# Batch normalisation, streamed: loads freed of their wait on VectorE while each store stays held for its predecessor's landing, VectorE's two instructions fused, ScalarE's share cut from 2048 to 1408 columns

One core of a Trainium2 chip. The metric is the device time of one execution in microseconds (us); lower is better.

## The reference

```python
# x: (32, 256, 128, 128) float32; gamma, beta, running_mean, running_var: (256,)
return gamma * (x - mean) / np.sqrt(var + eps) + beta      # per channel
```

Each element is read, scaled and shifted by two numbers of its channel, and written. 537 MB go in and 537 MB come out.

## The kernel before

x is cut into 64 tiles of 128 channels x 16384 columns (8 MB; 64 KB in each of 128 partitions). There are three buffers of a tile each (192 KB per partition together). SyncEngine issues the loads, ScalarE the stores, so they are on two DMA queues; VectorE scales columns 0 to 14335 in place, in two instructions, and ScalarE the last 2048. The parts that matter (`...` marks cuts):

```python
NBUF = 3
STEP, VCOLS, VLAST = 2560, 14336, 9216
...
for i in range(1, NT):                       # SyncEngine: loads
    s, turn = i % NBUF, i // NBUF
    if turn:
        nc.sync.wait_ge(stored[s], 16 * turn)            # store i-3 has left the buffer
    inst = nc.sync.dma_start(out=bufs[s][:], in_=xr[i]).then_inc(loaded[s], 16)
    if turn:
        inst._wait_ge(vdone, 2 * (i - 1) + 1)            # tile i-1 landed, its first 2560 columns done
...
for i in range(1, NT):                       # VectorE
    vector_part(i, 0, STEP)._wait_ge(*landed(i))
    vector_part(i, STEP, VLAST if i == last else VCOLS)
for i in range(last):                        # ScalarE: its columns, then the store
    nc.scalar.wait_ge(vdone, 2 * (i + 1))
    inst = scalar_part(i, VCOLS)
    if i:                                                # store i-1 has landed
        inst._wait_ge(stored[(i - 1) % NBUF], 16 * ((i - 1) // NBUF + 1))
    store(i)                                             # waits for scalar_part(i)
```

So there are two **holds**: a load is held for a piece of VectorE work on the tile loaded before it, a store for the landing of the store before it.

## Time and profile before

| | before |
|---|---|
| time, median of 3 runs | 2484.97 us |
| span of the profiled run | 2483.3 us |
| one tile (one load and one store), steady state | 38.68 us |
| moved | 1073.85 MB, 432 GB/s |

The prediction below shows the lines that carry the argument. Two more are needed for comparison, the DMA issues of the page (size, count, median us from issue to landing):

```profile
out_dram<-t ACTq DMA_DIRECT2D x64, 36.5
t<-in_x_dram SPq DMA_DIRECT2D x63, 37.0
```

Both are shorter than a tile's 38.68 us, so each queue is empty for a moment in every tile.

### The profile page before, as it was taken

The numbers are of one execution on the slowest core, as the hardware profiler recorded it, in microseconds if no ns is written. First come the engines' busy times: TensorE is split into PE (matmuls) and PEld (weight loads), VectorE is DVE, ScalarE is ACT, GpSimd is POOL, SyncE is SP. The second block draws the span as 40 slices with busy tenths as digits, with TensorE's granted clock in tenths as the row PEclk, the third lists the DMA queues.
The fourth block names the chain that finished last, engine by engine and source line by source line (L and its number), as shares of the span: only waits on it lengthen the run. The fifth ranks groups of instructions, "written<-read, shape, count | busy, mean of one in ns | idle before, by whom it ended". The sixth has DMA issues, their size and how long they took to land.

```text
span 2483.3 us, 516 instructions
## 1 busy us (share of the span) xinstructions
DVE 508.8 (20%) x139; ACT 139.8 (6%) x66; POOL 0.2 (0%) x4
## 2 busy tenths in 40 slices
DVE  3122121221212212122121221212212122121220
ACT  0000000000000000000000000000000000000001
POOL 0000000000000000000000000000000000000000
DMA  9999999999999999999999999999999999999999
GB/s 415 430 439 434 428 436 436 435 433 430 432 433 438 430 432 433 435 424 437 437 428 436 438 436 429 437 435 430 436 437 436 430 437 435 429 437 435 433 433 408
DMA packets 18708, 1073.85 MB, mean 432 GB/s; under 512 B 2128, under 2 KB 2192, under 8 KB 2192
## 3 DMA queue, kind: packets, MB, share of 16 engines
q1 hardware_dynamic: 9488, 536.94, 50.1%
q10 hardware_dynamic: 9216, 536.88, 49.9%
q14 instruction: 4, 0.03, 0.0%
HBM read 536.94 MB, written 536.87 MB: 432 GB/s over the span
## 4 chain that ended last, share of the span: by engine, by line
DMA 93%; DVE 4%; another core or an unknown queue 1%; ACT 0%; issue 0%; SPq 0%; DVEq 0%
DMA t<-in_x_dram 93%; DVE t L130 4%; ACT t L141 0%; SPq L91 0%; DVE rows L89 0%; SPq L95 0%; DVE eps_t L107 0%; DVEq L198 0%; SPq L70 0%
## 5 line engine op out<-in xcount | busy, mean ns | idle before, releaser
L130 DVE TENSOR_SCALAR t<-t,scale_t,shift_t 128x11776 f32<-128x11776 f32 (+2 forms) x128 | 505.3, 3989 | 1930.4 <-DMA t<-in_x_dram 1930.2
L141 ACT ACTIVATE t<-t,shift_t,scale_t 128x2048 f32<-128x2048 f32 x64 | 138.2, 2159 | 2299.3 <-DMA out_dram<-t 2276.6
L108 DVE STREAM_TRANSPOSE turned<-rows 32x1024 f32<-32x1024 f32 x1 | 1.2, 1233 | 12.5 <-DMA rows<-in_running_mean_dram 12.5
L115 ACT ACT_TABLE_LOAD x1 | 1.3, 1283 | 0.9 <-SPq L70 0.9
L89 DVE MEMSET rows<- 32x1024 f32 x1 | 0.9, 912 | 1.2 <-SPq L70 1.2
L115 ACT ACTIVATE std_t<-par,eps_t 128x2 f32<-128x2 f32 x1 | 0.3, 296 | 14.7 <-DVE par L113 14.7
L113 DVE COPY par<-turned 32x8 f32<-32x8 f32 x4 | 0.6, 161 | 0.1
L122 DVE RECIPROCAL rstd_t<-std_t 128x2 f32<-128x2 f32 x1 | 0.2, 166 | 0.4 <-ACT std_t L115 0.4
L125 DVE TENSOR_TENSOR shift_t<-par,ms_t 128x2 f32<-128x2 f32 x1 | 0.2, 161 | 0.0
L124 DVE TENSOR_TENSOR ms_t<-par,scale_t 128x2 f32<-128x2 f32 x1 | 0.2, 161 | 0.0
L123 DVE TENSOR_TENSOR scale_t<-par,rstd_t 128x2 f32<-128x2 f32 x1 | 0.2, 160 | 0.0
L187 POOL MEMSET const-bfloat16-1.0<- 128x1 bf16 x1 | 0.1, 101 | 0.0
L187 POOL MEMSET const-uint8-127<- 128x1 uint8 x1 | 0.1, 101 | 0.0
L187 POOL MEMSET const-float32-0.0<- 128x1 f32 x1 | 0.1, 98 | 0.2 <-issue 0.2
L187 POOL MEMSET const-float32-1.0<- 128x1 f32 x1 | 0.1, 98 | 0.0
L107 DVE MEMSET eps_t<- 128x1 f32 x1 | 0.1, 59 | 0.1
## 6 DMA issues: line engine op xcount, KB each, us to landing
t<-in_x_dram SPq DMA_DIRECT2D x2, 4096.0 KB, 16.5
out_dram<-t ACTq DMA_DIRECT2D x64, 36.5
t<-in_x_dram SPq DMA_DIRECT2D x63, 37.0
rows<-in_running_var_dram SPq DMA_DIRECT2D x1, 16.0 KB, 11.3
rows<-in_gamma_dram SPq DMA_DIRECT2D x1, 16.0 KB, 11.1
rows<-in_beta_dram SPq DMA_DIRECT2D x1, 16.0 KB, 10.9
rows<-in_running_mean_dram SPq DMA_DIRECT2D x1, 16.0 KB, 11.3
```

The costliest lines, as they stand in the source:

```text
L89: zeroed = step(nc.vector.memset(rows[:], 0.0))
L107: step(nc.vector.memset(eps_t[:], eps))
L108: step(nc.vector.transpose(out=turned[:], in_=rows[:]), fetched, 16 * NPAR)
L113: placed = step(nc.vector.tensor_copy(out=flat[q * B : (q + 1) * B], in_=blocks[:, :, q, 0]))
L115: nc.scalar.activation(out=std_t[:], in_=var_t, func=mybir.ActivationFunctionType.Sqrt, bias=eps_t[:], scale=1.0,)._wait_ge(vec, placed).t ...
L122: step(nc.vector.reciprocal(out=rstd_t[:], in_=std_t[:]), act, 1)
L123: step(nc.vector.tensor_mul(out=scale_t[:], in0=gamma_t, in1=rstd_t[:]))
L124: step(nc.vector.tensor_mul(out=ms_t[:], in0=mean_t, in1=scale_t[:]))
L125: ready = step(nc.vector.tensor_sub(out=shift_t[:], in0=beta_t, in1=ms_t[:]))
L130: return nc.vector.tensor_scalar(out=t[:, first:end], in0=t[:, first:end], scalar1=scale_t[:, cb : cb + 1], scalar2=shift_t[:, cb : cb + 1 ...
L141: return nc.scalar.activation(out=t[:, first:], in_=t[:, first:], func=mybir.ActivationFunctionType.Identity, bias=shift_t[:, cb : cb + 1] ...
L187: nc = _bacc.Bacc("TRN2", target_bir_lowering=False, num_devices=1)
```

## The change

It frees the loads of the wait on VectorE (985 us of SyncEngine's waiting), shortens the ScalarE pass that lies between two stores, and fuses VectorE's two instructions into one.

```diff
-STEP = 2560
-VCOLS = 14336
+VCOLS = 14976
...
-            if turn:
-                nc.sync.wait_ge(stored[s], 16 * turn)
             inst = nc.sync.dma_start(out=bufs[s][:], in_=xr[i]).then_inc(loaded[s], 16)
             if turn:
-                inst._wait_ge(vdone, 2 * (i - 1) + 1)
+                inst._wait_ge(stored[s], 16 * turn)
...
-            vector_part(i, 0, STEP)._wait_ge(*landed(i))
-            vector_part(i, STEP, VLAST if i == last else VCOLS)
+            vector_part(i, 0, VLAST if i == last else VCOLS)._wait_ge(*landed(i))
         for i in range(last):
-            nc.scalar.wait_ge(vdone, 2 * (i + 1))
+            nc.scalar.wait_ge(vdone, i + 2)
```

More of the change, by code (lines that the diff above doesn't have):

```diff
@@ L167 @@
         scalar_part(last, VLAST)._wait_ge(*landed(last))
-        nc.scalar.wait_ge(vdone, 2 * NT)
+        nc.scalar.wait_ge(vdone, NT + 1)
         store(last)
```

## The prediction

> **What bounds the kernel now.** I read the page first: what the engines and the DMA engines are busy with.
>
> ```profile
> DVE 508.8 (20%) x139; ACT 139.8 (6%) x66; POOL 0.2 (0%) x4
> ...
> DMA  9999999999999999999999999999999999999999
> ...
> HBM read 536.94 MB, written 536.87 MB: 432 GB/s over the span
> ...
> DMA t<-in_x_dram 93%; DVE t L130 4%; ACT t L141 0%; SPq L91 0%; DVE rows L89 0%; SPq L95 0%; DVE eps_t L107 0%; DVEq L198 0%; SPq L70 0%
> ```
>
> VectorE and ScalarE are mostly idle, and no slice of the DMA row falls below nine tenths. The chain that ended last names loads (93%) and the short VectorE piece between two loads (4%). That 4% looks like a loss to be won back. Whether it is one, the timeline of a steady stretch and the table of stretches tell:
>
> ```profile
> 1197.34 2.09 ACT L141 ACTIVATE t<-t,shift_t,scale_t 128x2048 f32<-128x2048 f32 x1 [36.50 <-DMA out_dram<-t]
> 1199.47 0.34 ACTq L154 DMA_DIRECT2D out_dram<-t  x1
> 1211.90 7.93 DVE L130 TENSOR_SCALAR t<-t,scale_t,shift_t 128x2560 f32<-128x2560 f32 x2 [30.69 <-DMA t<-in_x_dram]
> 1213.55 77.61 SPq L102 DMA_DIRECT2D t<-in_x_dram  x3
> 1236.02 2.09 ACT L141 ACTIVATE t<-t,shift_t,scale_t 128x2048 f32<-128x2048 f32 x1 [36.58 <-DMA out_dram<-t]
> ```
> ```profile
> 158.30:2399.00 2240.70, 460.26 (x116) 121.37 (x58) 0.00 (x0) 1.00 1.00 434
> ```
>
> From one ScalarE pass to the next is 1236.02 - 1197.34 = 38.68 us (38.64 averaged over the neighbours): one tile loaded and one stored. Both queues have a pause per tile: the store is released at 1199.47, the next load at 1213.55, 14 us apart, so one queue runs alone in the other's pause. In the records of single packets a tile is 8 packets of 64 KB per DMA engine and direction; a packet takes an engine 2.414 us from start to start, whether loads, stores or both are queued, and the next starts when it ends. 16 x 2.414 = 38.63 us, the whole period. So the DMA engines have no idle time at all in the steady state (the table's DMA share over 2240 us is 1.00, at 434 GB/s); the 4% of VectorE in the chain is hidden. 64 x 38.63 = 2472 us of the 2483 us span; the rest is start and end. **There is nothing above about 0.5% to win, whatever the waits are; a new idle moment of the DMA engines is a loss in full.**
>
> **What the Trainium skill says.** (1) "DMA: Bandwidth & Descriptors", section "Queues, rings and completion order": each DMA engine takes turns between queues, packet by packet. The packet records agree: where both have work, each engine alternates one load and one store packet. (2) The same page, "Why a DMA increments its semaphore by 16 and not by 1": the 16 engines finish independently and only the full count means that all has landed. Here one store's 16 completion marks lay from 1192.5 to 1197.0 us, 4.5 us apart, and ScalarE began 0.33 us after the last. (3) The same page, "Where 436 GB/s comes from", gives 435.2 GB/s as the ceiling; the 434 here agrees. (4) The same page, "Anatomy of one DMA", puts about 2 us of fixed cost on a DMA and says that any wait is done by the issuing sequencer, before dispatch. The trace shows the parts of it that matter here, which I use instead.
>
> **The change part by part.**
>
> *VectorE and ScalarE work.* Two VectorE instructions per tile become one of 14976 columns. From the groups by shape, 2560 columns take 1.613 us and 11776 take 6.408 us, so 0.520 ns per column and about 8.07 us for 14976, against 8.02 us now. ScalarE's 2048 columns take 2.093 us and the single 7168 take 6.360 us, so 0.833 ns per column: 1408 columns take 1.56 us, 0.53 us less. Neither engine bounds anything, and a tile will have been scaled about a period before its store. Worth nothing while the DMA engines are full.
>
> *The loads' pause goes.* A load now waits only for the store that empties its buffer (load i for store i-3), no longer for 2560 columns of the tile before it. That wait costs 985 us in total on SyncEngine (61 times 16.15 us), but it is not a loss: it is what puts loads half a turn away from stores.
>
> ```profile
> SPq L101 <- DMA out_dram<-t: 1398.1, 61, 68.8
> SPq L102 <- DVE t L130: 985.0, 61, 16.2
> ```
>
> *What this makes of the order.* Load i+3 and store i+1 are now released by the same event, the last landing of store i; the load at once, the store 1.56 us of ScalarE later. So loads get a lead in every turn, of ScalarE's time plus the store's start-up: in the trace the first store packet moves 3.6 us or more after its issue when loads are queued. That is about 1.6 + 3.6 = 5 us or two packets, in which loads run alone; then the queues alternate; the loads, 8 packets like the stores, run out first; the last two or so store packets go alone. When the slowest engine ends the store, nothing is queued anywhere: three buffers, of which one is just stored and two are loaded. **Both queues are empty until the landing has been seen and a new load has started.** A lead of a few loads at the start does not save it: load 2 has about 2 to 3 packets left per engine when store 0 ends (store 0's first packets move at 35 us, when 5 to 6 of load 1's 8 have gone; the remaining 10 to 11 against store 0's 8), and each pause of the stores consumes 2 to 3. It is gone by the end of store 1 or 2.
>
> *The size of the idle moment.* Last completion mark to seen: 0.33 us in the steady state, 0.36 us at the end of the kernel. Issue to moving bytes in an idle machine: only the first load shows it. Issued at 0.95 us, its first packet starts at 1.95 us, the slowest engine's at 2.56 us, and the first packets take 1.6 to 2.4 us where later ones of their size (32 KB) take 1.21 us. The slowest two engines end their first packet at 4.20 and 4.52 us, that is 2.04 and 2.36 us later than a packet's time after the issue. The table of stretches shows the silence:
>
> ```profile
> 0.95:1.90 0.95, 0.69 (x1) 0.95 (x1) 0.00 (x0) 1.00 0.00 0
> 1.90:2.90 1.00, 0.28 (x2) 0.28 (x1) 0.00 (x0) 1.00 1.86 524
> ```
>
> The slowest engine sets each turn. So 0.36 + 0.02 + (2.04 to 2.36) = 2.4 to 2.7 us; I take 2.45, as a first issue is probably slower than a later one. New period: 38.63 + 2.45 = 41.1 us.
>
> *Number and sum.* Stores 1 or 2 to 60 each release a load that way: 59 times 2.45 = 145 us. After store 61 no load is left, and store 62 comes after ScalarE as well: 0.36 + 1.56 + 2.1 = 4 us. The end (store 63 queued behind store 62) and the start (1408 instead of 2048 columns, -0.2 us) stay. 2485 + 145 + 4 = 2634 us; rounded 2632.
>
> **The rivals.**
>
> *The queues stay full.* If the loads kept a backlog over the end of each store, the idle moment would be covered and the time would stay at 2480 to 2490 us. For it: at the start there is a backlog, and the engines are up to 4.5 us out of step, so some have work when others are done. Against it: the alternation is one to one, the backlog can only shrink while stores alone pause, and a load can't be issued before a store frees its buffer. A strong preference of the DMA engines for stores would be needed; the packet records show none. I give it 7%.
>
> *The idle moment is longer.* The engines' being out of step could be paid too: if, in a turn, one engine is a whole packet (2.4 us) later than the others, everything waits for it, and the period would be 38.63 + 4.9 = 43.5 us, 2484 + 60 x 4.9 = 2780 us. For it: 4.5 us between first and last completion mark now. Against it: that spread is of whole packets by order of turns, and in the new order every engine has the same 16 packets between two common starts, with only the start's 0.6 us between engines. 7%.
>
> *The idle moment is shorter.* If a warm issue moves bytes in 1 us and the first packet costs no more than later ones, 0.36 + 1.0 + 0.1 = 1.5 us: 59 x 1.5 + 3 = 91 us, 2576 us. Quite possible; it sets my lower end.
>
> *A gain.* Two waits fewer in the chain might seem to give back 4%, 2390 us. That needs 452 GB/s over the whole span; no packet in the trace goes faster than 2.414 us. 1%.
>
> **Range and chances.** The shorter idle moment gives 2576 and a longer one of 3.4 us (start-up as measured plus another microsecond of packet fill) gives 2690. Range 2572 to 2690. Faster 1%, within 2% (up to 2535 us) 8%, slower 91%.
>
> **What the changed profile would show.** Right: the DMA share of a steady stretch near 0.94 and about 408 GB/s instead of 434; ScalarE passes about 41.1 us apart; each load issued within 0.1 us of the ScalarE pass beginning, both right after a store's landing; loads landing some packets before the store of the same turn, and then about 2.4 us in which no packet starts; SyncEngine waiting for stores alone. Wrong: passes 38.6 us apart with the share at 1.00 (first rival: loads still under way when a store ends), or 43 us apart (second rival: completion marks of a store still 4 us apart). The whole argument fails if store packets get more than every second turn while loads are queued, or if loads end after the stores.

## The result

The changed kernel takes **2710.69 us** (median of 4 runs, 2709.51 to 2713.30) against 2484.26 us: ratio 1.0916, 95% interval 1.0900 to 1.0932. (Ratios here are the mean time of one kernel's fast runs over that of the other's in the same rounds, so not quite the ratio of the medians.) The prediction had the direction and the mechanism, but 2632 us, with 2690 at the upper end.

The timeline of a steady stretch of the changed kernel (columns: start, duration, engine, line, operation; in brackets the idle time before it and what ended that):

```profile
1225.13 8.08 DVE L125 TENSOR_SCALAR t<-t,scale_t,shift_t 128x14976 f32<-128x14976 f32 x1 [34.95 <-DMA t<-in_x_dram]
1227.53 85.42 SPq L97 DMA_DIRECT2D t<-in_x_dram  x3
1227.54 1.56 ACT L136 ACTIVATE t<-t,shift_t,scale_t 128x1408 f32<-128x1408 f32 x1 [41.44 <-DMA out_dram<-t]
1229.13 0.34 ACTq L149 DMA_DIRECT2D out_dram<-t  x1
1268.01 8.08 DVE L125 TENSOR_SCALAR t<-t,scale_t,shift_t 128x14976 f32<-128x14976 f32 x1 [34.80 <-DMA t<-in_x_dram]
1270.42 1.56 ACT L136 ACTIVATE t<-t,shift_t,scale_t 128x1408 f32<-128x1408 f32 x1 [41.32 <-DMA out_dram<-t]
```

The load at 1227.53 and ScalarE's pass at 1227.54 are released by one landing. Before, they were 14 to 16 us apart. The load of the same turn had landed at 1225.13, when VectorE begins: 2.4 us before that store. At 1225.13 each DMA engine was at its last store packet; in the packet records the last of these ended at 1227.16, and no packet of the next tile started before 1228.48.

SyncEngine's waits (us in total, times, longest), the table of stretches (its last three columns are TensorE clock, DMA share, GB/s) and the page's DMA issues agree:

```profile
SPq L97 <- DMA out_dram<-t: 2596.7, 61, 66.9
```
```profile
158.30:2399.00 2240.70, 428.20 (x53) 82.74 (x53) 0.00 (x0) 1.00 0.95 396
```
```profile
out_dram<-t ACTq DMA_DIRECT2D x64, 40.6
t<-in_x_dram SPq DMA_DIRECT2D x63, 39.8
```

Note that the share fell by 5% and the rate by 9% (434 to 396 GB/s). **A busy share does not show that packets take longer**, and longer packets are the part of the loss that the prediction missed. The trace's records of single packets split a tile's time, for each DMA engine, into packets at the steady 2.414 us, what load packets took beyond 2.418 us (store packets took none), and time in which the engine had none (means over tiles 2 to 59, us):

| kernel | one tile | 16 packets x 2.414 | slow load packets | idle |
|---|---|---|---|---|
| before | 38.68 | 38.63 | 0.05 | 0.0 |
| changed | 42.31 | 38.63 | 1.66 | 2.0 |

The last completion mark of a store (each DMA engine writes one, a record of 4 bytes, when its share is done) is followed 1.33 us later by the first load packet on the first engine. The first load packet of a tile takes 3.08 us in the mean, the second 3.40, the other six 2.42.

The books close. Up to the landing of store 61 the changed kernel lost 231.7 us: 59 tiles by 3.63 = 214 us; 4.8 and 14.6 us more than a tile before in the first two periods, when the order collapses; -1.9 us at the first store. From there to the end it takes 43.5 us against 49.6, as its last load has long landed. 231.7 - 6.1 = 225.6 us, the difference of the spans.

### The profile page after: what moved, and what is told of

Same layout as the page of the kernel before. It is cut to its first block, busy times and chain, and to the rows that moved or that the text cites. A ratio compares the mean times of both kernels' runs of the same rounds, so it can differ in the third digit from the quotient of the medians.

```text
span 2708.9 us, 392 instructions
## 1 busy us (share of the span) xinstructions
DVE 517.9 (19%) x76; ACT 106.3 (4%) x66; POOL 0.2 (0%) x4
## 2 busy tenths in 40 slices
DMA packets 18708, 1073.85 MB, mean 396 GB/s; under 512 B 2128, under 2 KB 2192, under 8 KB 2192
## 3 DMA queue, kind: packets, MB, share of 16 engines
q1 hardware_dynamic: 9488, 536.94, 49.6%
## 4 chain that ended last, share of the span: by engine, by line
DMA 93%; ACT 4%; another core or an unknown queue 1%; DVE 0%; issue 0%; SPq 0%; ACTq 0%; DVEq 0%
DMA out_dram<-t 90%; ACT t L136 4%; DMA t<-in_x_dram 3%; DVE t L125 0%; SPq L90 0%; DVE rows L88 0%; ACTq L149 0%; DVE eps_t L102 0%; DVEq L192 0%; ACTq L156 0%; SPq L69 0%
## 5 line engine op out<-in xcount | busy, mean ns | idle before, releaser
L125 DVE TENSOR_SCALAR t<-t,scale_t,shift_t 128x14976 f32<-128x14976 f32 (+2 forms) x65 | 514.4, 7913 | 2136.4 <-DMA t<-in_x_dram 2136.3
L136 ACT ACTIVATE t<-t,shift_t,scale_t 128x1408 f32<-128x1408 f32 x64 | 104.7, 1636 | 2552.5 <-DMA out_dram<-t 2541.3
```

The lines of the kernel that those rows point to most:

```text
L125: return nc.vector.tensor_scalar(out=t[:, first:end], in0=t[:, first:end], scalar1=scale_t[:, cb : cb + 1], scalar2=shift_t[:, cb : cb + 1 ...
L136: return nc.scalar.activation(out=t[:, first:], in_=t[:, first:], func=mybir.ActivationFunctionType.Identity, bias=shift_t[:, cb : cb + 1] ...
```

## The experiments

**Theory (coinciding releases):** one event, the landing of a store, now releases both the next load and, after ScalarE, the next store; both queues run empty together once per tile, and the DMA engines, which are the bound, stand still. **Rivals:** the new split of work, or the fused VectorE instruction, costs; ScalarE's pass is on the path, as the chain of the changed kernel has 4% of it; three buffers are too few. Every timed run below is against the kernel before of its own rounds.

### 1. cols_only: the split of columns alone

```diff
 # kernel before
-VCOLS = 14336
+VCOLS = 14976
```

> The kernel before with only the column split of the change (VectorE ends at column 14976, ScalarE takes 1408); both waits stay. Theory of empty queues (the period grew because loads and stores are now released by one event, so that both queues run empty once per tile): within 0.5% of the kernel before, 2475 to 2495 us, period 38.6 us. Rival, that the new split of the work costs or gains time by itself: more than 1% off, towards 2710 us if it is the whole cause.

2487.46 us, ratio 1.0009 (0.9994 to 1.0024). The split is nothing.

### 2. load_wait_only: the load's wait alone

```diff
 # kernel before
-            if turn:
-                nc.sync.wait_ge(stored[s], 16 * turn)
...
-                inst._wait_ge(vdone, 2 * (i - 1) + 1)
+                inst._wait_ge(stored[s], 16 * turn)
```

> The kernel before with only the load's wait changed: no wait for 2560 columns of the preceding tile, the landing of the store of three tiles earlier alone; two VectorE instructions and 2048 ScalarE columns stay. Theory of empty queues: the whole loss is here, 2690 to 2730 us, period about 42.3 us. Rival, that the fused VectorE instruction or the new split carries a part: clearly less than 2690 us.

2716.51 us, ratio 1.0936 (1.0920 to 1.0953); 42.39 us per tile, of which 1.64 us slow load packets and 2.05 us idle. The whole loss is in this one wait, with VectorE's two instructions and ScalarE's 2048 columns still there.

### 3. store_late: ScalarE's pass 5.2 us longer

```diff
 # changed kernel
-VCOLS = 14976
+VCOLS = 8704
```

> The changed kernel with 7680 instead of 1408 ScalarE columns per tile, so about 6.8 instead of 1.56 us between the landing of a store and the issue of the next one; VectorE's pass shrinks to about 4.8 us. Theory of empty queues: the store's pause is covered by the load that starts at once, so the period stays at 42.3 us (2690 to 2730 us) if the slow first two load packets (3.08 and 3.40 us instead of 2.42) are a property of a cold start; about 1 us per tile less (2640 to 2665 us) if the second slow packet comes from the store's issue or from VectorE's pass at that moment. Rival, reading the 4% of ScalarE in the chain of the changed kernel as time on the path: plus 5.2 us per tile, about 3030 us.

2719.66 us, ratio 1.0951 (1.0933 to 1.0969), so within about 0.35% of the changed kernel (1.0916): the time of the first reading (its reason falls below), and the rival of ScalarE on the path falls. Yet the chain that ended last now says, by engine, for this kernel:

```profile
DMA 82%; ACT 16%; issue 0%; DVE 0%; SPq 0%; ACTq 0%; DVEq 0%
```

and for the changed kernel:

```profile
DMA 93%; ACT 4%; another core or an unknown queue 1%; DVE 0%; issue 0%; SPq 0%; ACTq 0%; DVEq 0%
```

The chain follows one store to the next. It does not see that ScalarE's 6.79 us lie beside load packets, and that a store which starts later has fewer load packets to take turns with. A share in the chain is no price.

The single packets tell more than the time. The second load packet is back at 2.42 us, but a later one is slow instead, by about 1.1 us per engine: the packet just ahead of the store's first packet (12.73 us after the landing, 7.72 in the changed kernel). VectorE was not running then. So this microsecond **moves with the store's start**; it is not tied to the load's second packet, nor to VectorE's pass.

### 4. cold_parts: the two start-ups by themselves

```diff
 # changed kernel; VectorE's and ScalarE's work on tiles dropped, result wrong on purpose
             inst = nc.sync.dma_start(out=bufs[s][:], in_=xr[i]).then_inc(loaded[s], 16)
-            if turn:
-                inst._wait_ge(stored[s], 16 * turn)
+            inst._wait_ge(loaded[(i - 1) % NBUF], 16 * ((i - 1) // NBUF + 1))
...
+        # ScalarE: when all loads have landed, each store waits for the landing of the one before
```

> Wrong result on purpose, to measure the start-up alone: all 64 loads one after another, each issued when the one before has landed, then all 64 stores likewise, no VectorE or ScalarE work. If the slow fill is a property of a cold load: period of a load 19.3 + 1.3 + 1.65 + about 0.5 = 22.8 us, first packets 3.1 and 3.4 us. If it comes from the store issued 1.6 us later or from VectorE: first packet about 3.1, second 2.42, period about 21.8 us. Stores: 19.3 + 1.4 + 0.1 + 0.3 = 21.1 us.

A load takes 21.87 us: 8 x 2.414 = 19.31 and 2.56 us of **restart**, as all time beyond the packets' own is called here, slow packets included. Its first packet takes 3.08 us, all others 2.42: the second reading. A store takes 20.78 us, with a restart of 1.47 us and a first packet of 2.46 us. So a load that starts on idle DMA engines costs 2.56 us, close to the 2.45 us of the prediction; the slow packet of experiment 3 comes on top, where a store joins.

### 5. both_free: the store's hold gone as well

```diff
 # changed kernel
-            inst = scalar_part(i, VCOLS)
-            if i:
-                inst._wait_ge(stored[(i - 1) % NBUF], 16 * ((i - 1) // NBUF + 1))
+            scalar_part(i, VCOLS)
             store(i)
```

> The changed kernel without the store's hold: ScalarE takes its 1408 columns as soon as VectorE has done its part, and the store is queued behind its predecessor. Theory of empty queues: when a store ends, the next one is already queued, so the DMA engines never run empty while a load starts; period 38.63 us, 2475 to 2500 us, and no slow load packets. Rival, that freely queued loads are the fault by themselves (the waits on loads being what the kernel before needed): stays above 2600 us.

2501.87 us (2489.88 to 2516.81), ratio 1.0086 (1.0035 to 1.0137): a shade above the expected range, but nine tenths of the loss is gone. The period is 38.83 us, with no idle time and 0.18 us of slow load packets. (These are from the profiled run of 2493.0 us; the four runs lie in two pairs, near 2491 and near 2514 us, and why is not known.) Free loads are not the fault by themselves. The DMA issues of its page show how it stays full:

```profile
out_dram<-t ACTq DMA_DIRECT2D x64, 47.2
t<-in_x_dram SPq DMA_DIRECT2D x63, 59.7
```

Both are longer than a tile's time: on each queue the next transfer is there before the last has ended.

### 6. six_halves: half tiles in six buffers

```diff
 # changed kernel
-NBUF = 3
+NBUF = 6
-VCOLS = 14976      # and VLAST 9216 -> 4608
+VCOLS = 7488
-    HW = H * W
-    NT = N * NCB
+    HW = H * W // 2
+    NT = N * NCB * 2
... (the addresses of a load and a store follow)
```

> The changed kernel with tiles of half the columns in six buffers of half the size, waits unchanged (a load for the buffer's store, a store alone for its predecessor). Theory of empty queues: buffers do not help, because loads run ahead until all are full and then wait for the very store that the next store waits for; the idle moment comes 128 times: 19.4 + 3.5 = 22.9 us per half tile, 2880 to 2980 us. Rival, that three buffers are too few and a deeper supply of loads would cover the store's hold: about 2484 to 2600 us.

2891.52 us, ratio 1.1637 (1.1620 to 1.1655); 22.88 us per half tile. More buffers do not help: loads run ahead until every buffer waits for the same store, and the stop comes twice as often. Six halves hold no more bytes than three whole tiles, though; a supply deeper in bytes was not tried.

### 7. load_hold_back: a load's hold again, but a whole tile of VectorE work

```diff
 # changed kernel
+            if turn:
+                nc.sync.wait_ge(stored[s], 16 * turn)
             inst = nc.sync.dma_start(out=bufs[s][:], in_=xr[i]).then_inc(loaded[s], 16)
             if turn:
-                inst._wait_ge(stored[s], 16 * turn)
+                inst._wait_ge(vdone, i + 1)
```

> The changed kernel with the load's second wait put back, now for the whole VectorE pass of the preceding tile (8.1 us, as it is one instruction). Theory of empty queues: loads start half a turn from stores again, so one queue works in the other's pause; period 38.6 to 39.8 us, 2480 to 2560 us, although each load is held longer than in the kernel before. Rival, that a wait in front of loads costs time: at least as slow as the changed kernel, or 6.5 us per tile more, about 3100 us.

3056.99 us, ratio 1.2300 (1.2280 to 1.2321): a clear miss. The timeline:

```profile
1193.48 8.08 DVE L127 TENSOR_SCALAR t<-t,scale_t,shift_t 128x14976 f32<-128x14976 f32 x1 [39.95 <-DMA t<-in_x_dram]
1201.58 96.98 SPq L99 DMA_DIRECT2D t<-in_x_dram  x3
1201.65 1.56 ACT L138 ACTIVATE t<-t,shift_t,scale_t 128x1408 f32<-128x1408 f32 x1 [46.47 <-DVE t L127]
```

ScalarE no longer waits for a store but for VectorE: the end of a VectorE pass (1201.56) releases the next load and the store of that very tile. Queues that once were half a turn apart have found another common event, and stand still for about VectorE's 8.08 us (idle 7.9 us per engine and tile in the mean, with 1.65 us of slow load packets besides). The table of stretches:

```profile
158.30:2399.00 2240.70, 371.63 (x46) 71.73 (x46) 0.00 (x0) 1.00 0.84 348
```

The theory survives in a wider form, **any** common event will do, which experiments 13 and 14 put to the test; my belief that a hold on loads keeps the queues apart by itself does not.

### 8. start_together: load and store issued at the same moment

```diff
 # changed kernel: stored[...] is waited for ahead of the load, and the load waits for
+                inst._wait_ge(adone, i - 1)      # ScalarE's columns of the store to come
```

> The changed kernel with the load held until ScalarE's 1408 columns are done, so that load and store are issued at the same moment after the landing. Two readings of the second slow load packet of the changed kernel: if it is the start of a store upon 16 engines that all work on loads that costs it (0.98 us), it goes when both start together: 38.63 + 1.33 + 1.60 + 0.67 + 0.69 = 42.9 us, about 2750 us. If it belongs to any start: 43.9 us, about 2812 us.

3347.99 us, ratio 1.3467 (1.3447 to 1.3487), 52.9 us per tile: neither reading. Packets are slow all through the tile, not only at its start: load packets 3.70 us for the first, 2.99 in the mean of the later ones, store packets 2.59; engines end a store 5.9 us apart. Of the 14.3 us beyond 38.63, slow load packets are 5.3, slow store packets 1.4, and idle engines 7.6. Why, stays open.

### 9. step_longer: the load's hold 3.5 instead of 1.6 us

```diff
 # kernel before
-STEP = 2560
+STEP = 6144
```

> The kernel before with the load held for 6144 instead of 2560 columns of the preceding tile, about 3.5 instead of 1.6 us (the whole tile at once, 8.1 us, collapsed into common starts in an earlier run of this study). Theory of coinciding releases: a hold costs nothing as long as a load's cycle (hold plus flight) fits into the DMA engines' 38.63 us, because then stores and loads keep being released by different events; the flight can shrink to about 32 us (3.7 us to its first packet, 4.4 packets alone, 3.6 in turns), so up to some 6.5 us fits: within 1% of the kernel before, 2475 to 2510 us. Rival, that a hold adds its length: plus 1.9 us per tile, about 2600 us.

2582.85 us, ratio 1.0402 (1.0374 to 1.0430): a miss. Who waited for whom, in the kernel before and in this one:

```profile
ACT t L141 <- DMA out_dram<-t: 2276.6, 62, 44.8
```
```profile
ACT t L141 <- DVE t L130: 2225.6, 59, 41.0
...
ACT t L141 <- DMA out_dram<-t: 146.9, 4, 43.0
```

The releases are like those of load_hold_back: with the longer hold, stores wait for the tile just loaded, so the landing of a load releases both. The loss is of another make. The DMA engines hardly stand still:

```profile
158.30:2399.00 2240.70, 444.38 (x112) 115.38 (x56) 0.00 (x0) 1.00 0.99 416
```

Of the 1.5 us that a tile takes longer than before (40.19 us), 1.2 us are slow load packets, mostly the packet just ahead of a store's first one (3.2 us in the mean), and about 0.4 us are idle. So slow packets come without both queues running empty.

The kernel before was balanced: 1.6 us of hold before each load, 2.1 us before each store. That this balance is what matters is argued; no run lengthened both holds together. My reckoning that 6.5 us of hold would fit was wrong. It let a load's flight (issue to landing) shrink to 32 us; it took 38.0 us here.

### 10. store_free_only: only the store's hold removed

```diff
 # kernel before
-            inst = scalar_part(i, VCOLS)
-            if i:
-                inst._wait_ge(stored[(i - 1) % NBUF], 16 * ((i - 1) // NBUF + 1))
+            scalar_part(i, VCOLS)
```

> The kernel before with its load's hold kept and the store's hold on its predecessor removed; the fourth corner of the two holds. Theory of coinciding releases: the queues never run empty together, 2475 to 2510 us. Rival, that freely queued stores fall in step with loads: above 2550 us.

2562.96 us, ratio 1.0318 (1.0298 to 1.0338): above the expected range and in the rival's. With experiment 5 the four corners are (ratio to the kernel before):

| | store held | store free |
|---|---|---|
| load held | 1 (2484 us) | 1.032 |
| load free | 1.092 | 1.009 |

Neither hold is good or bad. With both, the queues pause at different times; with none, each has its next transfer waiting; with one alone, their releases meet. In this run stores wait for VectorE 63 times, and loads and stores are again tied to one landing of a load (1.6 and 10 us after it). As in experiment 9, the engines stay busy:

```profile
158.30:2399.00 2240.70, 444.36 (x112) 117.17 (x56) 0.00 (x0) 1.00 0.99 418
```

A tile takes 40.16 us, 1.2 us of it slow load packets and about 0.3 us idle. The expectation, that the queues never run empty together, nearly held; that the time would stay did not.

### 11 and 12. store_swapped, start_together_swapped: the store in two halves, upper partitions first

```diff
 # changed kernel, and start_together; waits on stored doubled to 32
-            nc.scalar.dma_start(out=outr[i], in_=bufs[s][:])._wait_ge(adone, i + 1).then_inc(stored[s], 16)
+            for n, rows_ in enumerate((slice(64, 128), slice(0, 64))):
+                inst = nc.scalar.dma_start(out=outr[i][rows_], in_=bufs[s][rows_])
...
```

> The changed kernel with each store issued as two transfers of 64 partitions, the upper half first[...]. If the slow load packet ahead of a store's first packets (0.98 us per tile) comes from load and store working on like rows at the same time, it goes: packets of 2.42 us, period about 41.4 us, 2640 to 2670 us. If it comes from the store's start on engines in step, whatever the rows: unchanged, 2690 to 2730 us.

> The kernel whose load and store are issued together (52.9 us per tile, packets of 2.6 to 3.7 us all through the tile) with the same swap of the store's halves. If like rows at the same time are what slows the packets: packets near 2.42 us and a period of 42.9 to 43.9 us, 2750 to 2820 us. If the common start itself does it: stays above 3200 us.

3243.16 us (ratio 1.3062) and 3337.56 us (1.3434). Inconclusive as to the times: a 64 KB packet of a 64-partition store took 5.11 us on an engine when nothing else was queued, instead of 2.42, so the edit brought in a cost of its own. As to the packets, the first load packets were still slow (3.10 and 3.18 us in store_swapped), and later ones too. No record shows which rows an engine is at, so that the swap made them unlike is not shown. Nothing speaks for like rows as the cause, and nothing rules them out.

### 13 and 14. drain_every_8, drain_every_2: the common event put into the kernel before

```diff
 # kernel before (8, and the same with 2)
             if turn:
                 nc.sync.wait_ge(stored[s], 16 * turn)
+            if turn and i % 8 == 0:
+                nc.sync.wait_ge(stored[(i - 2) % NBUF], 16 * ((i - 2) // NBUF + 1))
```

> The kernel before, except that every eighth load (8 to 56, seven of them) also waits for the store that releases the next store, so that both queues run empty together there and nowhere else. Theory of coinciding releases with the cost per event read from the changed kernel (1.95 us of idle DMA engines and 1.71 us of slow load packets, 3.7 us): plus 7 x 3.7 = 26 us, about 2510 us, slow load packets only in the tiles after such a load. If one event throws the order of the queues off for good, as the longer hold and the free stores did, the periods stay above 40 us and the time is 2560 us or more.

> The same with every second load (4 to 62, thirty of them). Cost per event of 3.7 us: plus 111 us, about 2595 us; with the order thrown off for good: no more than in the run with seven such loads, or more than 2650 us with gaps of both kinds.

2542.51 us (ratio 1.0237, 1.0220 to 1.0254) and 2695.94 us (1.0853, 1.0837 to 1.0869): 8.4 and 7.1 us per event (58.5 / 7, 212 / 30), twice what I expected. The trace shows why. One such load (load 16), in us between landings of stores:

| store after the event | one tile | idle | slow load packets |
|---|---|---|---|
| ahead of it | 33.8 | 1.5 | 0.1 |
| first | 42.9 | 2.4 | 1.8 |
| second | 46.7 | 0.9 | 1.8 |
| third | 39.7 | 0 | 0.2 |
| fourth and on, to the next event | 38.6 | 0 | 0 |

(The tile ahead held 13 packets per engine instead of 16, the second one 19.)

and the timeline of another one (load 40):

```profile
1566.29 2.09 ACT L143 ACTIVATE t<-t,shift_t,scale_t 128x2048 f32<-128x2048 f32 x1 [31.72 <-DMA out_dram<-t]
...
1606.09 7.93 DVE L132 TENSOR_SCALAR t<-t,scale_t,shift_t 128x2560 f32<-128x2560 f32 x2 [41.52 <-DMA t<-in_x_dram]
1614.12 2.09 ACT L143 ACTIVATE t<-t,shift_t,scale_t 128x2048 f32<-128x2048 f32 x1 [45.74 <-DVE t L132]
...
1654.91 2.09 ACT L143 ACTIVATE t<-t,shift_t,scale_t 128x2048 f32<-128x2048 f32 x1 [38.70 <-DMA out_dram<-t]
```

One event leads to a second one: the late load is also late for its store, which for once waits for VectorE (1614.12). After that the old order comes back by itself. So the loss is per event, it does not throw the order off for good, and slow load packets come with such restarts: in the tiles between them they are at 0.0 to 0.4 us. The cost of 8.4 us is two restarts of about 4 us.

## Why the prediction was right in kind and wrong in size

- **The bound.** Right: nothing to win from the waits; none of the thirteen correct variants beat the kernel before.
- **The columns.** Right: 8.08 and 1.56 us per pass, as worked out; no effect on the time (experiment 1).
- **The common release.** Right: load and ScalarE's pass 0.01 us apart, both on a store's landing, and the whole loss in this one wait (experiment 2). The backlog of loads was gone by the landing of store 2 (counted from 0), as said. One store packet ran alone at the end, not "two or so".
- **The size of the idle moment: the step that failed.** It read "0.36 + 0.02 + (2.04 to 2.36) = 2.4 to 2.7 us; I take 2.45", with all of the start-up from the kernel's first load, on which no store follows for 28 us. That much is what a load restarting alone costs (2.56 us, experiment 4). In the changed kernel a restart costs 3.66 us: 2.0 us of idle and 1.66 us of slow load packets, of which 0.67 us is the first packet and 0.98 us is the packet ahead of the store's start. The missing term is that last one; the prediction had "another microsecond of packet fill" only as its upper end. 59 x (3.66 - 2.45) = 71 us, which takes 2632 to 2703 of the 2711 us. I could have seen it: in the kernel before, at 32 us, the load packets just ahead of store 0 took 2.7 to 3.6 us. I had read the packets of the steady state and of the very start, and not those.
- **The rest.** The collapse of the order cost 14.6 us in one tile, which I did not foresee. In that tile load and store packets are slow throughout (4.7 and 1.7 us in sum per engine) and the engines end the store 5.4 us apart, as in experiment 8. The end was put at +4 us and came out at -6. Two slips of the sums change nothing: 2634 was "rounded" to 2632, and 1073.85 MB in 2390 us need 449 GB/s, not 452.
- **The rivals.** Full queues: no. "Longer", for engines out of step by a packet: the period is near (42.3 against 43.5 us), but not for that reason, as a store's completion marks are now 0.9 us apart.
- **Of what the profile would show:** the share of 0.94 came as 0.95, but 408 GB/s came as 396. That gap was the slow packets.

Open: why the start of a store slows the load packet ahead of it by a microsecond in the changed kernel, and in experiments 9 and 10 with hardly any idle time before it, but not in the steady state of the kernel before; why a common issue (experiment 8) slows packets throughout; and what exactly lets a load's flight shrink no further (experiment 9). A pointer for the first, not a cause: over eleven runs that packet took 3.4 us where the 16 engines began it nearly in step (standard deviation of the starts under 0.25 us, 361 stores) and 2.6 us where they were out of step (0.6 us or more, 207 stores); store_free_only goes against it, with 3.2 us out of step.

## What to carry to other kernels

When the DMA engines are the bound, ask of every pair of queues which event ends each one's pause: if it was the same event, the engines stood still or ran slow packets in every case here, and neither more, smaller buffers nor a shorter or longer compute pass between mended it. Two cures are shown: pauses that are ended by different events, as in the kernel before (a fragile order, as a hold 1.9 us longer broke it), and the next transfer queued before the last ends on both queues. Compare a transfer's time to landing with the time of a tile to see which you have. A wait that a profile shows as long can be what keeps two queues apart, and a share in the chain can lie beside other work: change its length before you pay for it.

## What the Trainium skill lacked or had wrong

- "DMA: Bandwidth & Descriptors", "Anatomy of one DMA — SWDGE (gpsimd) path": its 2 us of fixed cost are for DMAs issued from GpSimd. Here SyncEngine and ScalarE issue them; the idle time per restart was 2.0 us in the changed kernel, which does not test that figure. It lacks that the packets after a restart are slow too: first load packet 3.08 instead of 2.42 us, and the packet ahead of a store that joins 3.40 us; 3.66 us per restart in all.
- The same page, "Queues, rings and completion order": it has the turns between queues, and the trace shows them; it lacks how late a newly issued transfer gets its first turn when another queue is at work: 3.6 to 5.7 us after the issue for stores in the kernel before.
- No page has it that two queues released by one event run dry together: 9.2% here, 16.4% with half tiles.
